# Layer 0 of a two-layer encoder: values first, rotary tables built once per frequency, first weights through ScalarE's queue

## Chip, cores, metric

One core of one Trainium2 chip. The metric is the device time of one execution in microseconds (us), the median of several runs. Engines are named as in the profile: PE (TensorE matmul), PEld (its weight loads), DVE (VectorE), ACT (ScalarE), POOL (GpSimd), SP (SyncE, which issues most DMAs).

## The reference

Batch 1, 256 tokens, width 2048, two layers. Each layer normalizes, projects once, runs two head groups and adds the output projection to the residual:

```python
for l in range(DEPTH):
    h = rms_norm(x, norm_g[l])
    proj = jnp.einsum('btd,dc->btc', h, w_in[l])
    rw_in, g_rw, q, k_at, v_at, g_at = jnp.split(proj, col_splits, axis=-1)
    rw_in = bidir_token_shift(rw_in, shift_mu[l])
    r, k, v, xw, xa = jnp.split(rw_in, rw_splits, axis=-1)
    y_rw = rwkv7_branch(r, k, v, xw, xa, ...)          # scans in both directions, 16 heads of 64
    qh = rope(q.reshape(B, T, AT_HEADS, HEAD_DIM), positions)
    kh = rope(k_at.reshape(B, T, AT_KV_HEADS, HEAD_DIM), positions)
    vh = v_at.reshape(B, T, AT_KV_HEADS, HEAD_DIM)
    y_at = window_attention(qh, kh, vh, sink[l])       # |i-j| <= 128, 4 kv heads, 16 query heads
    mix = jnp.concatenate([y_rw * silu(g_rw), y_at * silu(g_at)], axis=-1)
    x = x + jnp.einsum('btc,cd->btd', mix, w_out[l])
return rms_norm(x, final_g)
```

`rope` needs the sine and cosine of position times one of 32 frequencies, for every token.

## The kernel before

**Weights.** Each weight tile is read as 128x1024 `raw` (SP's queue, three buffers), split by ACT into `hi` (L253) and by DVE into the rest `lo` (L255), 512 columns at a time, two buffers of each. X is split likewise into `XH` (ACT L217) and `XL` (DVE L218), with the norm's gain `G0` multiplied in. A *step* multiplies one 128-row block of a tile by X in three matmuls (L331 to L333, or L600 to L602 for the attention values, where X is the stationary operand). An input tile of 128 columns has 16 steps, the values 32, so a layer has 864 input steps, then 256 output steps.

**The stream.** `S.add` queues a tile's steps, `S.run(n)` emits the next n; `S.later(n, f)` calls f after n more steps. When two steps of a half tile are left, the next half's split is emitted. Only PE keeps the order in which the program is written; DVE, ACT and SP instructions are placed by a scheduler by priority, and those called through `PA` and `PV` keep their order among themselves.

**Layer 0's start.** Eleven matmuls on zeros (L1185) warm PE up. The first tiles are the decay input (`xw`) and the in-context-rate input (`xa`). After the 16 X tiles the squares are summed into `ACC` (four 1024-wide squares on ACT, three adds on DVE), and `norm.add` (L230) turns ACC into the norm by matmuls with a column of ones, eight of them. `norm.spread` (L238) gives the row `rb` that evacuations multiply by.

**Windows.** A layer then runs 13 windows of 64 steps in 11 slots each; between the steps of a slot, generators are advanced. Window w starts head pair w (tiles k, v, r, gate): `scan_p(w)` prepares it, `scan_i` (windows w+2, w+3) builds an inverse in small matmuls, whose pieces pass through ACT (`QF`, `tt`) and DVE (`tv`), `scan_b` (w+3, w+4) runs the scan. The value, key, query and gate tiles of the attention follow the pairs. The generator `attend()` has 17 pieces, placed by `ATT`: `scores(j)` (matmuls into `pscr`, softmax on DVE and ACT into a buffer of tag `mv`), `flip(j)` (transposes `ppt`), `values(j)` (matmuls `po`). In layer 0 the generator `setup()` is advanced at the slots of `ROT`: masks and constants, and then the rotary angles, reduced to a small range in many 128x256 DVE instructions, one piece each, in windows 2 to 7; ACT makes `SIN` and `COS` in window 7.

Of the kernel before, what the change touches and what calls it, by code (L numbers as in the profile page):

```python
# [133 lines left out]
def hybrid_trunk_kernel(ctx, tc, xT, wi, wv, wo, par, fing, dup, iup, sink, pos, cst, out):  # L134
# [209 lines left out]
    SY.dma_start(out=first_w[0][:, 0:512], in_=wi[0, 0, 0, :, 0:512])
    SY.dma_start(out=G0, in_=par[0, :, P_NG : P_NG + NKT])
# [18 lines left out]
    COS = cp.tile([128, T], F32, name="COS")  # L364
    SIN = cp.tile([128, T], F32, name="SIN")

    def setup():
# [6 lines left out]
        for l in range(DEPTH):  # L374
            s = DP[:, l, 0:NSH]
            V.tensor_tensor(s, PR[:, l, P_MU0 : P_MU0 + NSH], PR[:, l, P_MU1 : P_MU1 + NSH], op=ALU.add)
# [30 lines left out]
        def reduce_by(dst, src, period, bits, shift):  # L407
            PV.tensor_scalar(nn, src, 1.0 / period, shift, op0=ALU.mult, op1=ALU.add)
            yield
            PV.tensor_scalar(nn, nn, MAGIC, MAGIC, op0=ALU.add, op1=ALU.subtract)  # L410
            yield
# [893 lines left out]
```

## Time and profile before

| what | value |
|---|---|
| median of 3 runs | 1169.26 us (1168.23 to 1169.78) |
| the profiled execution's own time | 1168.46 us |
| its span, first to last instruction | 1166.7 us |
| mean granted PE clock | 0.994 |
| PE, DVE, ACT busy share | 98%, 79%, 67% |

A row of stretches reads: from:to in us, length, then busy us and instruction count of PE, PEld, DVE, ACT, POOL, then the granted PE clock, the DMA engines' busy share and GB/s. A timeline row reads: start, duration, engine, line, operation, tile written <- tiles read, shape, count, and in brackets the idle time before it and what ended it. Matmuls overlap in the pipeline: a 128x256 one lasts 0.28 us in the record while they start 0.12 apart.

### The profile page before, as it was taken

How to read it: one execution, taken by the hardware profiler on the slowest of the kernel's cores; microseconds unless marked ns; L12 is line 12 of the kernel's file. 1: busy time of each engine (PE TensorE's matmuls, PEld its weight loads, DVE VectorE, ACT ScalarE, POOL GpSimd, SP SyncE). 2: the span in 40 equal slices, each digit the busy share in tenths (PEclk: the TensorE clock that was granted, in tenths of full speed). 3: DMA queues.
4: the chain of work that ended last, by engine and by line, in shares of the span. 5: the costliest groups of instructions: out<-in, count | busy, mean ns of one | idle time of the engine just before them, and what ended most of it. 6: DMA issues, size and time to landing. Idle time of an engine off the chain costs nothing.

```text
span 1166.7 us, 37155 instructions
## 1 busy us (share of the span) xinstructions
PE 1145.5 (98%) x15671; PEld 1051.1 (90%) x15671; DVE 915.9 (79%) x2042; ACT 785.6 (67%) x1986; POOL 21.7 (2%) x23
## 2 busy tenths in 40 slices
PE   8999999999999999999999999999999999999996
PEld 7998999999899998988899889999999999988885
DVE  7889978888877677767768888888887767786665
ACT  6667876787775666655556677876786666675553
POOL 0000000000000000000000000000000000000000
PEclk9999999999999999999999999999999999999998
DMA  7544434333334443477655443334333344345663
GB/s 261 169 152 134 131 103 130 97 112 111 101 116 123 126 127 122 133 235 242 217 182 171 143 136 116 100 114 126 104 112 112 120 130 130 101 150 184 211 202 126
DMA packets 60551, 166.59 MB, mean 143 GB/s; under 512 B 7744, under 2 KB 22880, under 8 KB 60384
## 3 DMA queue, kind: packets, MB, share of 16 engines
q1 hardware_dynamic: 60384, 164.21, 45.1%
q8 instruction: 123, 2.02, 0.7%
q14 instruction: 44, 0.36, 0.1%
HBM read 157.37 MB, written 4.19 MB: 138 GB/s over the span
## 4 chain that ended last, share of the span: by engine, by line
PE 76%; issue 13%; DVE 5%; ACT 4%; DMA 2%; SPq 0%; POOL 0%; POOLq 0%; DVEq 0%; ACTq 0%
PE pm L331 17%; PE pm L333 14%; PE pm L332 14%; PE pm L324 4%; PE pg L855 3%; PE pm L325 2%; PE pcc L1018 2%; DVE lo L255 2%; PE pcc L1046 2%; PE pd L962 1%; PE py L1030 1%; PE py L1003 1%; PE pq L953 1%; PE pcc L1036 1%; ACT hi L253 1%
## 5 line engine op out<-in xcount | busy, mean ns | idle before, releaser
L255 DVE TENSOR_TENSOR lo<-raw,hi 128x512 fp32r<-128x512 f32 x560 | 371.9, 686 | 103.7 <-ACT hi L253 101.6
L253 ACT ACTIVATE hi<-raw 128x512 fp32r<-128x512 f32 x560 | 329.5, 625 | 167.8 <-PE pm L324 58.4
L331 PE MATMUL pm<-XHa,hi 128*128 128x256 f32 x832 | 245.5, 295 | 0.9 <-ACT VA L609 0.4
L331 PE MATMUL pm<-XHb,hi 128*128 128x256 f32 x832 | 243.6, 293 | 0.2 <-ACT hi L253 0.2
L333 PE MATMUL pm<-XHb,lo 128*128 128x256 f32 x832 | 234.0, 281 | 1.4 <-DVE lo L255 1.4
L333 PE MATMUL pm<-XHa,lo 128*128 128x256 f32 x832 | 234.2, 281 | 1.1 <-DVE lo L255 0.8
L332 PE MATMUL pm<-XLa,hi 128*128 128x256 f32 x832 | 234.2, 282 | 0.5 <-DVE XLa L218 0.3
L332 PE MATMUL pm<-XLb,hi 128*128 128x256 f32 x832 | 234.0, 281 | 0.1
L331 PEld LDWEIGHTS pm<-XHa,hi 128*128 128x128 f32 x832 | 157.0, 189 | 11.6 <-ACT XHa L217 1.7
L324 PE MATMUL pm<-M,hi 128*128 128x512 f32 x480 | 166.9, 392 | 0.4 <-ACT hi L253 0.4
L331 PEld LDWEIGHTS pm<-XHb,hi 128*128 128x128 f32 x832 | 157.2, 189 | 5.9 <-ACT hi L253 0.4
L333 PEld LDWEIGHTS pm<-XHa,lo 128*128 128x128 f32 x832 | 157.2, 189 | 2.4 <-DVE lo L255 2.3
L333 PEld LDWEIGHTS pm<-XHb,lo 128*128 128x128 f32 x832 | 157.2, 189 | 2.1 <-DVE lo L255 2.0
L332 PEld LDWEIGHTS pm<-XLa,hi 128*128 128x128 f32 x832 | 157.3, 189 | 1.1 <-DVE XLa L218 1.1
L332 PEld LDWEIGHTS pm<-XLb,hi 128*128 128x128 f32 x832 | 157.3, 189 | 0.3 <-DVE XLb L218 0.3
L325 PE MATMUL pm<-M,lo 128*128 128x256 f32 x480 | 134.3, 280 | 0.2 <-DVE lo L255 0.2
L324 PEld LDWEIGHTS pm<-M,hi 128*128 128x128 f32 x480 | 90.1, 188 | 21.2 <-issue 0.8
L325 PEld LDWEIGHTS pm<-M,lo 128*128 128x128 f32 x480 | 90.1, 188 | 0.5 <-DVE lo L255 0.5
L1041 ACT ACTIVATE suv<-pcc 64x128 f32<-64x128 f32 x128 | 34.5, 270 | 72.3 <-PE pcc L1039 48.5
L1124 ACT ACTIVATE mv<-mv,mx 128x257 f32<-128x257 f32 x56 | 28.0, 502 | 15.1 <-DVE mx L1121 15.0
L956 ACT ACTIVATE QF<-pq 128x256 f16<-128x256 f32 x80 | 30.4, 380 | 10.5 <-PE pq L920 6.2
L855 PE MATMUL pg<-mv,FR 64*128 64x128 f32 x512 | 37.2, 285 | 0.0
(292 smaller groups left out, 2044.3 us busy)
## 6 DMA issues: line engine op xcount, KB each, us to landing
raw<-wi SPq DMA_DIRECT2D x207, 512.0 KB
raw<-wo SPq DMA_DIRECT2D x64, 512.0 KB
raw<-wv SPq DMA_DIRECT2D x8, 512.0 KB
rrot<-u SPq DMA_DIRECT2D x80, 32.0 KB
vg<-xT SPq DMA_DIRECT2D x16, 128.0 KB
xd<-vg SPq DMA_DIRECT2D x16, 128.0 KB
vg<-xd SPq DMA_DIRECT2D x16, 128.0 KB
g<-dup SPq DMA_DIRECT2D x16, 97.0 KB
```

The source lines that it names most:

```text
L253: A.activation(hi[:, q], raw[:, q], AF.Copy)
L255: V.tensor_tensor(lo[:, q], raw[:, q], hi[:, q].bitcast(F32), op=ALU.subtract)
L324: PE.matmul(pm, wh, m.row(kk), start=(kk == 0), stop=(kk == 15), skip_group_check=True)
L325: PE.matmul(pm[:, 0:T], wl, m.row(kk, 0), start=False, stop=(kk == 15), skip_group_check=True)
L331: PE.matmul(pm, wh, xh, start=(kk == 0), stop=False)
L332: PE.matmul(pm, wh, xl, start=False, stop=False)
L333: PE.matmul(pm, wl, xh, start=False, stop=(kk == 15))
L855: PE.matmul(pg[:, h, c * 128 : (c + 1) * 128], BK[half[h], d, c, 1 - h : 3 - h, :].rearrange("p s j -> p (s j)"), MV[half[h], d, c].rearra ...
L956: A.activation(t_sub(QF), flat4(pq[:, :, 0:128]), AF.Copy)
L1018: PE.matmul(pc[half[h], 0, d, :], GE[h][r, d, ci[d], 0, :], SUV[r, d, ci[d], h, :], start=True, stop=True)
L1041: A.activation(here(h), pc[half[h], 1], AF.Copy)
L1124: A.activation(Sc[:, h, q, 0:257], Sc[:, h, q, 0:257], AF.Exp, scale=0.125, bias=mx[:, q : q + 1], accum_out=den[:, q : q + 1])
```

## The change

Four things move together, and then the windows and their tables are laid out anew:

- In layer 0 the four value tiles come first, then xw and xa, then pair 0. Each X tile now serves two value steps (one per 128 tokens), and the evacuation of the values waits 23 steps. xw and xa go to the two halves of one `ps_w` bank pair. In layer 1 the values come right after xw and xa. So 64 steps precede window 0 instead of 32, and 12 windows of 64 and one of 32 follow.
- The first half tile of values and G0 are issued on ACT's queue.
- `setup()` keeps program order throughout (`PV`, `PA`). Positions are loaded as 32x64 quarters, so that partitions hold 4 blocks of tokens times 32 frequencies: the angles are 128x64 instead of 128x256, the sine's and the cosine's arguments are reduced together as 128x128, one Sin makes both, and 16 small DMAs spread the table to `TRIG` (128 x 2 x 256). The Sin stands in window 1; the copies in windows 2 and 3.
- ACC is folded twice more on DVE (to 512 and to 256 columns), and `norm.add` takes one sum instead of four: two matmuls instead of eight, after step 50.

```diff
 ATT = [
-    [3, 9],
-    [1, 3, 5, 6, 8, 10],
-    [0, 2, 4, 5, 6, 8, 9, 10],
+    [9],
+    [1, 4, 8],
+    [0, 2, 3, 5, 6, 8, 9],
+    [0, 1, 2, 3, 4],
 ]
-ROT = {0: [2, 3], 1: [], 7: [2, 5, 7], 8: [1, 3], 9: []}
+ROT = ([2, 4, 6, 7, 9], [3], [3, 5, 8], [2, 6], [5])
...
-    SY.dma_start(out=first_w[0][:, 0:512], in_=wi[0, 0, 0, :, 0:512])
-    SY.dma_start(out=G0, in_=par[0, :, P_NG : P_NG + NKT])
+    A.dma_start(out=first_w[0][:, 0:512], in_=wv[0, 0, :, 0:512])
+    A.dma_start(out=G0, in_=par[0, :, P_NG : P_NG + NKT])
     for a, b in ((0, 2), (2, 4), (4, 8), (8, 12), (12, 16)):
         SY.dma_start(out=X0[:, a:b, :], in_=xT[:, a:b, :])
...
+        if a in (2, 4):
+            SY.dma_start(out=first_w[a // 2], in_=wv[0, a // 2])
...
-        yield from reduce_by(ang, ang, two_pi * 4096.0, 7, 0.0)
-        for dst, shift, add in ((SIN, 0.0, 0.0), (COS, 0.25, np.pi / 2)):
-            yield from reduce_by(dst, ang, two_pi, 11, shift)
...
+        reduce_by(AN[:, 0:1], AN[:, 0:1], two_pi * 4096.0, 7, nn[:, 0:1], (0.0,))
         yield
+        reduce_by(table, AN[:, 0:1].to_broadcast([128, 2, 64]), two_pi, 11, nn, (0.0, 0.25))
+        PV.tensor_scalar(table[:, 1], table[:, 1], float(np.pi / 2), None, op0=ALU.add)
+        PV.tensor_scalar(table, table, PI_IN, -PI_IN, op0=ALU.min, op1=ALU.max)
+        yield
+        PA.activation(table, table, AF.Sin)
...
+        for i, q in enumerate(quarter):
+            for r in quarter:
+                SY.dma_start(out=TRIG[r, :, i * 64 : (i + 1) * 64], in_=table[q])
+            yield
...
+        turns = [(k, b) for k in range(4) for b in range(2)] if l == 0 else [(k, b) for b in range(2) for k in range(4)]
+        done = (lambda: S.later(23, v_evac)) if l == 0 else v_evac
...
         if l == 0:
-            inproj(0, lambda pm: S.later(29, lambda: xw_evac(pm)), raws=first_w, bank=lambda: wbank("pm")[:, 0:T])
-            inproj(1, lambda pm: S.later(13, lambda: xa_evac(pm)))
+            values_in()
...
+            inproj(0, lambda pm: S.later(13, lambda: xw_evac(pm)), bank=lead_bank(0))
+            inproj(1, lambda pm: S.later(4, lambda: xa_evac(pm)), bank=lead_bank(1))
         else:
             inproj(0, xw_evac)
             inproj(1, xa_evac)
+            values_in()
...
-            Sc = t["S"] = st("ge", [2, 2, 264], bufs=2) if j == 2 else st("mv", [2, 2, 264], bufs=3)
+            Sc = t["S"] = hold("s0b", F32, "S0", (2, 2, 264)) if j == 0 else st("mv", [2, 2, 264], bufs=3)
...
-        window(64, *scans(NP + 2), (att, ATT[0]))
-        window(64, *scans(NP + 3), (att, ATT[1]))
-        window(64, (att, ATT[2]))
+        for i in range(3):
+            window(64, *scans(NP + 1 + i), (att, ATT[i]))
+        window(32, (att, ATT[3]), groups=len(ATT[3]))
...
-    S.later(20, lambda: L0.norm.add([ACC[:, i * T : (i + 1) * T] for i in range(4)]))
-    S.later(27, lambda: L0.norm.spread())
+    PV.tensor_tensor(ACC[:, 0 : 2 * T], ACC[:, 0 : 2 * T], ACC[:, 2 * T : 4 * T], op=ALU.add)
+    PV.tensor_tensor(ACC[:, 0:T], ACC[:, 0:T], ACC[:, T : 2 * T], op=ALU.add)
+    S.later(18, lambda: L0.norm.add([ACC[:, 0:T]]))
+    S.later(25, lambda: L0.norm.spread())
```

Lines below 47 shift by one and more in the changed file: L253 becomes L254, L217 L218, L268 (everything called through `PA` or `PV`) L269.

ACT at the program's start, before, from its first instruction (`hi` is a weight split, `XH` an X tile, `mv` a sum of squares):

```order
L253 ACT_TABLE_LOAD
L253 ACTIVATE hi<-raw 128x512
L217 ACTIVATE XHa<-X0a,G_87 128x256
L253 ACTIVATE hi<-raw 128x512
L217 ACTIVATE XHa<-X0a,G_87 128x256 x7
L253 ACTIVATE hi<-raw 128x512 x2
L217 ACTIVATE XHb<-X0b,G_87 128x256 x8
L253 ACTIVATE hi<-raw 128x512 x2
L268 ACTIVATE mv<-X0a 128x1024 x2
```

ACT at the same place, now:

```order
L345 DMA raw<-wv 128x512
L346 DMA G_88<-par 128x16
L254 ACT_TABLE_LOAD
L254 ACTIVATE hi<-raw 128x512
L218 ACTIVATE XHa<-X0a,G_88 128x256
L254 ACTIVATE hi<-raw 128x512
L218 ACTIVATE XHa<-X0a,G_88 128x256 x3
L254 ACTIVATE hi<-raw 128x512 x2
L218 ACTIVATE XHa<-X0a,G_88 128x256 x4
L254 ACTIVATE hi<-raw 128x512 x2
L218 ACTIVATE XHb<-X0b,G_88 128x256 x8
L254 ACTIVATE hi<-raw 128x512 x4
```

Two DMA issues stand ahead, six weight splits instead of four are done before the last eight X tiles, and four more come before the squares.

DVE after the last X tiles, before (`lo` is a weight split, `mv` an add into ACC, `DP` a derived parameter of `setup()`):

```order
L218 SCALAR_TENSOR_TENSOR XLb<-X0b,G_87,XHb 128x256 x8
L255 TENSOR_TENSOR lo<-raw,hi 128x512 x2
L268 TENSOR_TENSOR mv<-mv 128x1024
L376 TENSOR_TENSOR DP<-PR 128x26
L379 TENSOR_SCALAR DP<-PR 128x8
L268 TENSOR_TENSOR mv<-mv 128x1024
L255 TENSOR_TENSOR lo<-raw,hi 128x512 x2
L268 TENSOR_TENSOR mv<-mv 128x1024
```

DVE there, now, up to the norm's first instruction (`rt`):

```order
L219 SCALAR_TENSOR_TENSOR XLb<-X0b,G_88,XHb 128x256 x8
L256 TENSOR_TENSOR lo<-raw,hi 128x512 x4
L269 TENSOR_TENSOR mv<-mv 128x1024 x2
L256 TENSOR_TENSOR lo<-raw,hi 128x512 x2
L269 TENSOR_TENSOR mv<-mv 128x1024
L256 TENSOR_TENSOR lo<-raw,hi 128x512
L269 TENSOR_TENSOR mv<-mv 128x512
L256 TENSOR_TENSOR lo<-raw,hi 128x512
L269 TENSOR_TENSOR mv<-mv 128x256
L269 TENSOR_TENSOR DP<-PR 128x26
L256 TENSOR_TENSOR lo<-raw,hi 128x512
L233 TENSOR_SCALAR rt<-pr 128x2
```

Two more weight splits precede the adds, and two narrow adds stand between later weight splits.

ACT around the sines, before, in window 7 (`suv` belongs to a scan, `QF` and `tt` to an inverse):

```order
L268 ACTIVATE FR<-FR 64x8x64
L1041 ACTIVATE suv<-pcc 64x2x64 x2
L268 ACT_TABLE_LOAD
L268 ACTIVATE SIN<-SIN 128x256
L268 ACTIVATE COS<-COS 128x256
L956 ACTIVATE QF<-pq 128x2x32x4
L924 ACTIVATE tt<-pq 128x2x64x2
```

ACT around the sines, now, in window 1 (`pp` and `ip` are decay factors of pair 0, `kr` an evacuated tile, `th`, `t` and `mf` prepare pairs 0 and 1):

```order
L269 ACTIVATE pp<-FR 128x512
L269 ACTIVATE ip<-FR 128x512
L254 ACTIVATE hi<-raw 128x512 x2
L478 ACTIVATE kr<-u,DP 128x256
L269 ACT_TABLE_LOAD
L269 ACTIVATE KA<-KA 128x128
L254 ACTIVATE hi<-raw 128x512
L269 ACTIVATE th<-th,DP 128x512
L269 ACTIVATE t_973<-kr,PR 128x256
```

The table load and the Sin now stand among weight splits and the preparation of a pair; no piece of an inverse is near.

More of the change, by code (lines that the diff above doesn't have):

```diff
@@ L363, in hybrid_trunk_kernel @@
     SK = cp.tile([128, DEPTH * 16], F32, name="SK")
-    COS = cp.tile([128, T], F32, name="COS")
-    SIN = cp.tile([128, T], F32, name="SIN")
+    TRIG = cp.tile([128, 2, T], F32, name="TRIG")
+    SIN, COS = TRIG[:, 0], TRIG[:, 1]
     def setup():
-        posi = st("t1", [T], I32, bufs=3)
-        SY.dma_start(out=posi, in_=pos.to_broadcast([128, T]))
+        posi = st("t1", [64], I32, bufs=3)
+        quarter = [slice(i * 32, (i + 1) * 32) for i in range(4)]
+        for i, q in enumerate(quarter):
+            SY.dma_start(out=posi[q], in_=pos[:, i * 64 : (i + 1) * 64].to_broadcast([32, 64]))
         SY.dma_start(out=FG, in_=fing)
@@ L402, in setup, with reduce_by @@
-        V.tensor_copy(ang, posi)
-        yield
+        AN = st("KA", [6, 64])
+        ang, nn, table = AN[:, 0], AN[:, 2:4], AN[:, 4:6]
+        PV.tensor_copy(ang, posi)
         PV.tensor_scalar(ang, ang, C[:, C_OFF["inv"] : C_OFF["inv"] + 1], None, op0=ALU.mult)
         yield
[L407 to L411, printed above, removed]
+        def reduce_by(dst, src, period, bits, n, shifts):
+            for i, shift in enumerate(shifts):
+                PV.tensor_scalar(n[:, i], src[:, 0], 1.0 / period, shift, op0=ALU.mult, op1=ALU.add)
+            PV.tensor_scalar(n, n, MAGIC, MAGIC, op0=ALU.add, op1=ALU.subtract)
@@ L589, in rope_evac @@
             return evac
-        pvs = []
-        def v_step(kk, b):
-            def f(w):
-                if not pvs:
-                    pvs.extend(ps_main.tile([128, T], F32, tag="m", name="pva") for _ in range(2))
-                k = kk % 4
-                wh, wl = (x[:, k * 256 : (k + 1) * 256] for x in w)
-                tb = slice(b * 128, (b + 1) * 128)
-                PE.matmul(pvs[b], L.XH[:, kk, tb], wh, start=(kk == 0), stop=False)
-                PE.matmul(pvs[b], L.XH[:, kk, tb], wl, start=False, stop=False)
-                PE.matmul(pvs[b], L.XL[:, kk, tb], wh, start=False, stop=(kk == 15))
-            return f
-        def v_evac():
-            L.VA = st("VA", [2, 256])
-            with tc.high_priority(offset=PRIO_B):
-                A.activation(L.VA[:, 0, :], pvs[0], AF.Copy, scale=L.norm.rt[:, 0:1])
-                V.tensor_scalar(L.VA[:, 1, :], pvs[1], L.norm.rt[:, 1:2], None, op0=ALU.mult)
-        for qt in range(4):
-            S.add(
-                lambda qt=qt: wsplit(wload(wv[l, qt])),
-                [v_step(qt * 4 + k, b) for k in range(4) for b in range(2)],
-                v_evac if qt == 3 else None,
-            )
         def k_place(m):
@@ L1190, in hybrid_trunk_kernel @@
         x_split(L0.XH, L0.XL, X0[:, k, :], k, 0)
-        S.run(1)
+        S.run(2)
+        if k == 11:
+            SY.dma_start(out=C, in_=cst[:, 0:C_KEEP])
+            SY.dma_start(out=PR, in_=par.rearrange("l p n -> p l n"))
     ACC = st("mv", [4 * T], bufs=3)
@@ L1215, in hybrid_trunk_kernel @@
         if l + 1 < DEPTH:
[L1216 removed]
+            S.run(64)
     end.norm.add(end.sums)
```

104 lines of the change are left out of this document (65 added, 39 removed).

## Prediction

> **What bounds the kernel.** I read the page first. TensorE is busy almost throughout, so a gain can come only from places where it waits or runs slowly.
>
> ```profile
> PE 1145.5 (98%) x15671; PEld 1051.1 (90%) x15671; DVE 915.9 (79%) x2042; ACT 785.6 (67%) x1986; POOL 21.7 (2%) x23
> ```
>
> Second, busy time by stretch, one stretch for each window of 64 weight steps (a step is three 128x256 matmuls). Layer 0's windows 0, 1, 5 and 7 and the sum of its thirteen come first, then layer 1's windows 0, 1, 5, 7 and sum. Both layers run the same work there, except that layer 0 also runs `setup()`, and in window 0 its norm.
>
> ```profile
> 23.70:50.20 26.50, 26.50 (x229) 26.50 (x228) 21.50 (x58) 16.36 (x34) 0.81 (x1) 1.00 0.62 201
> 50.20:77.40 27.20, 26.05 (x227) 25.24 (x225) 25.76 (x49) 19.22 (x43) 0.00 (x0) 1.00 0.50 158
> ...
> 187.20:228.10 40.90, 40.39 (x752) 37.32 (x751) 35.07 (x76) 30.51 (x82) 1.31 (x1) 1.00 0.37 113
> ...
> 268.20:311.50 43.30, 41.49 (x753) 38.52 (x751) 35.65 (x75) 33.86 (x86) 1.31 (x1) 0.96 0.37 115
> ...
> sum 471.80, PE 467.39 PEld 433.44 DVE 387.29 ACT 334.12 POOL 10.52; mean PE 35.95 PEld 33.34 DVE 29.79 ACT 25.70 POOL 0.81
> ```
> ```profile
> 599.30:623.50 24.20, 24.20 (x208) 24.20 (x207) 17.15 (x33) 14.57 (x30) 0.00 (x0) 1.00 0.61 184
> 623.50:651.10 27.60, 26.04 (x227) 25.23 (x225) 25.62 (x48) 19.22 (x43) 0.00 (x0) 1.00 0.51 156
> ...
> 760.60:800.50 39.90, 39.90 (x752) 37.06 (x752) 34.03 (x71) 30.40 (x82) 1.31 (x1) 1.00 0.37 112
> ...
> 840.50:880.30 39.80, 39.80 (x752) 36.97 (x751) 34.70 (x73) 30.42 (x82) 1.31 (x1) 1.00 0.37 113
> ...
> sum 465.10, PE 462.81 PEld 429.56 DVE 375.74 ACT 328.77 POOL 9.63; mean PE 35.60 PEld 33.04 DVE 28.90 ACT 25.29 POOL 0.74
> ```
>
> Layer 1 is the control: window 7 costs 3.5 us more in layer 0 (43.3 against 39.8), window 5 1.0 more, window 1 0.4 less. Third, the timeline and stretches around window 7's excess. The step is read here too: twelve matmuls start from 291.83 to 293.12, so 0.117 us each and 0.352 a step.
>
> ```profile
> 291.83 0.28 PE L331 MATMUL pm<-XHa,hi 128*128 128x256 f32 x1
> ...
> 293.12 0.28 PE L333 MATMUL pm<-XHa,lo 128*128 128x256 f32 x1
> 295.21 0.30 PE L962 MATMUL pd<-QF,tt 64*64 64x32 f16 x16 [1.81 <-ACT tt L924]
> ```
> ```profile
> 292.47 1.28 ACT L268 ACT_TABLE_LOAD   x1
> 293.76 0.42 ACT L268 ACTIVATE SIN<-SIN 128x256 f32<-128x256 f32 x1
> ```
> ```profile
> 292.50:295.90 3.40, 1.59 (x40) 1.37 (x38) 3.19 (x9) 3.36 (x10) 0.00 (x0) 1.00 0.25 61
> 295.90:299.30 3.40, 3.40 (x25) 3.24 (x21) 2.61 (x8) 3.36 (x11) 0.00 (x0) 0.50 0.25 101
> ```
>
> ScalarE loads a table and makes the sines just when the inverse needs `tt`; TensorE stands for 1.81 us, and then runs 3.4 us at a granted clock of 0.50, which costs another 1.7.
>
> Fourth, the start: timeline rows in time order by engine, then stretches (all engines; then the third matmul of each step alone, L333, whose count gives the steps; one record lies across a boundary).
>
> ```profile
> 0.74 0.38 SPq L344 DMA_DIRECT2D raw<-wi  x1
> 1.18 0.42 SPq L345 DMA_DIRECT2D G<-par  x1
> 5.46 0.55 PE L1185 MATMUL warm<-QF 128*128 128x512 f16 x1
> 6.37 0.38 PE L331 MATMUL pm<-XHa,hi 128*128 128x256 f32 x1 [0.36 <-ACT XHa L217]
> 8.96 1.71 ACT L217 ACTIVATE XHa<-X0a,G 128x256 fp32r<-128x256 f32 x4 [0.75 <-DMA X0a<-xT]
> 10.57 1.13 ACT L253 ACTIVATE hi<-raw 128x512 fp32r<-128x512 f32 x2
> 12.43 3.25 DVE L218 SCALAR_TENSOR_TENSOR XLb<-X0b,G,XHb 128x256 fp32r<-128x256 f32 x8
> 15.60 1.28 DVE L255 TENSOR_TENSOR lo<-raw,hi 128x512 fp32r<-128x512 f32 x2
> 15.85 1.99 ACT L268 ACTIVATE mv<-X0a 128x1024 f32<-128x1024 f32 x2
> 17.88 1.22 DVE L268 TENSOR_TENSOR mv<-mv 128x1024 f32<-128x1024 f32 x1 [1.00 <-ACT mv L268]
> 19.02 0.18 DVE L376 TENSOR_TENSOR DP<-PR 128x26 f32<-128x26 f32 x1
> 21.09 0.38 PE L333 MATMUL pm<-XHb,lo 128*128 128x256 f32 x1 [1.22 <-DVE lo L255]
> 25.19 1.84 PE L230 MATMUL pr<-C,mv 128*128 128x1 f32 x16
> ```
> ```profile
> 5.00:10.00 5.00, 4.09 (x16) 2.22 (x14) 2.87 (x7) 3.38 (x8) 0.00 (x0) 0.92 0.97 351
> 10.00:15.00 5.00, 4.91 (x29) 4.68 (x28) 4.96 (x12) 5.00 (x13) 0.00 (x0) 0.74 1.02 411
> ```
> ```profile
> 16.20:23.93 7.73, 4.71 (x17) 3.04 (x17) 1.00 0.57 191
> 23.93:37.46 13.53, 8.96 (x33) 6.03 (x33) 1.00 0.54 186
> ```
>
> Today 32 steps are done at 23.93 and 64 at 37.46. At 0.352 a step, 64 steps are 22.5 us; the rest is the 6.37 before the first step, waits, and the norm.
>
> **The front, worked out.** The old order gives TensorE one step (0.352) for each tile of X, while ScalarE spends 1.71/4 = 0.43 on it and VectorE 3.25/8 = 0.41. Values first gives two steps (0.70) a tile. Split costs are 0.57 (ScalarE) and 0.64 (VectorE) per 512 columns, so 32 value steps need about 11.4 us on ScalarE, 11.7 on VectorE, 11.3 on TensorE: balanced, and more bytes are wanted early, 4.1 MB before the last value step.
> The first matmul cannot come before the eleven warm matmuls end at 6.01: that gain is at most 0.36. The transfer that completes the first 1.55 MB ended a wait at 8.96 (X tiles 4 to 7; now it is the second half-megabyte of values). At 411 GB/s each further 0.52 MB takes 1.28. Moving two issues to ScalarE's queue brings X forward by nothing to 0.80 (0.38+0.42); I take 0.4, the middle. Then land: weights at 8.55, X4-7 9.85, weights 11.1, X8-15 13.7, weights 15.0, and after C and PR (0.46 MB, some of it in small packets) the decay tile at 17.5.
> ScalarE then does 4 X tiles 9.85-11.55, split to 12.7, 8 X tiles to 16.0, split to 17.15. VectorE's last value `lo` halves end at 17.25 and 17.9. Four steps follow each half: 17.25+1.3, then 1.4 more, so 32 steps are done near 20.0 instead of 23.93.
> Next, the squares come later than today. ScalarE: decay split 17.5-18.65, three squares to 21.6, half a split, the fourth square to 23.1. VectorE: adds of 1.22 until 23.0, `lo` to 23.6, where TensorE wants it at 23.05: wait 0.55. The third add ends near 25.6, then two new folds (0.65 and 0.35 by width) between `lo` splits end at 27.8. The norm's matmuls stand at step 50, which TensorE reaches at 26.9: a new wait of 0.9. They fall from eight to two, 1.84 to 0.46. The remaining 14 steps and the spread's matmuls bring step 64 to about 34.4. That is 3.1 earlier; I book 2.7, since C and PR's small packets may delay the decay tile. Ends: 1.0 (that delay at a further 2 us) and 4.5 (0.80 of shift, no wait at the norm).
>
> The Trainium skill ("DMA: Bandwidth & Descriptors", Issuing engines are not separate DMA queues) says that issuing from several engines only saves the sequencer's issue time. By that rule the shift would be the whole 0.80, and the sum -6.3 instead of -5.9; no run yet shows ScalarE's queue here.
>
> **Windows 1 to 7.** The layers' differences in window sums are 471.8-465.1 = 6.7, of which window 0 has 2.3 (norm and late evacuations, booked above). The remaining 4.4 lie in windows 1 to 7 and should go, since the sines leave the stretch in which inverses run: -4.4.
>
> The Trainium skill ("TensorE: Matmul & The Clock Gate", What you observe and the table of states) puts the return to half clock after at least one idle window of about 3.4 us. By that rule the 1.81 us stall would cost itself alone, and the sum would be -4.2. The trace disagrees: 0.50 was granted after a stretch that was busy 1.59 of 3.40 us.
>
> **What comes back.** The sines now stand in window 1, where no inverse runs, behind the split of half 16. ScalarE loads the table (1.28), works on 128 instead of 512 columns, and loads back later. Behind it wait the next weight splits. It is hidden if the split runs a half (2.8 us) ahead; at worst it costs 1.81+1.7 as above. I take 0.6.
> Seventeen angle instructions enter window 0 on VectorE, at 0.18 each (the DP row is nearest in width): up to 3.1, less the band cast that leaves. 21.5 busy becomes about 24 of a window that shrinks to some 24.5, and window 1 is already at 25.76 of 27.2. Ends: 0 and 2.4; I take 0.8, because splits have priority.
> SyncE gets 19 more issues (16 table copies, 3 for positions), 0.4 each. It mostly waits for buffers, as the first row shows, so I cost them at nothing; if a copy waited for late sines, the weight loads behind it would start late.
>
> ```profile
> SPq L245 <- DVE lo L255: 477.1, 164, 7.7
> ...
> PE pm L331 <- ACT VA L609: 0.4, 2, 0.2
> ```
>
> The second row is TensorE's wait for a value evacuation. In layer 0 the values' banks now come free at step 55, before step 65 wants them: -0.2. Layer 1 keeps its wait.
> Attention starts one window earlier and its end is denser, 32 steps for five pieces. The tightest score today, in timeline rows:
>
> ```profile
> 480.99 0.39 PE L1109 MATMUL pscr<-KA,kr 64*128 64x256 f32 x2
> ...
> 486.65 0.62 DVE L1127 TENSOR_SCALAR mv<-mv,den 128x256 f32<-128x256 f32 x2
> ...
> 492.59 0.60 PE L1136 MATMUL ppt<-C,mv 128*128 128x128 f32 x4
> ```
>
> It is ready 5.3 us before its transposes. Four slots become three, each of 6.4 steps (2.25) plus about 1.1 of small matmuls: 10.1 instead of 11.6, slack near 3.8. I cost it at 0, ends -0.5 and +2.
>
> Sum: -2.7 - 4.4 + 0.6 + 0.8 - 0.2 = -5.9. The profiled execution took 1168.46 (span 1166.7); it becomes 1162.6. The median of the three runs is 1169.26, 0.8 above it, so the forecast there is 1163.4.
>
> **Rivals.** (1) The sines stall TensorE in window 1 as they did in window 7: 3.5 instead of 0.6, +2.9 on the forecast, 1166.3. For it: the load is as long, VectorE there is 95% busy. Against: no `tt` is awaited there. (2) The front gains nothing: bytes, squares and the folds hold step 64 at 37.4. For it: the 0.97-1.02 DMA share from 5 to 15 us. Against: twice the matmuls per X tile. 1166.1. (3) The other side: attention becomes bound by latency. If window 11's seven pieces and the five of window 12 crowd VectorE so that the 5.3 us slack falls below zero, each of seven transposes in two layers waits; at 0.9 us each that is +12.6, giving about 1176. It decides once the lost slack passes 5.3 plus 0.4 a transpose (0.43 x 14 equals the gain of about 6). Against it: VectorE is below 80% over the span. (4) The change of order does nothing but shift the same waits: sines' 4.4 gone, the same lost at window 0 and 1 on VectorE; 1167 to 1169.
>
> **Chances.** Forecast 0.70, (1) 0.10, (2) 0.08, (4) 0.06, (3) 0.06. The range joins the favourable end (-4.5 - 4.4 - 0.2 - 0.5, about 1159.5) with the case of both new waits at their upper parts and a front of 1.0 (about 1168). About 0.2% (2.3 us) is what a measurement can tell from no change, so under 1166.9 counts as faster: the forecast, and most of (1) and (2), 0.83. Same 0.10, slower 0.07.
>
> **What would show it.** First step near 6.0; step 32 near 20 and step 64 near 34.4; two norm matmul pairs of about 0.5 with a wait on VectorE's ACC; layer 0's windows 5 and 7 within 0.3 of layer 1's; no granted 0.50 near 290; transposes of scores without waits. The forecast is wrong if window 0 or 1 grows by over 2 us, or if waits appear before the score transposes.

## The result, and the profile after

The changed kernel takes 1160.55 us (median of 6 executions, 1160.06 to 1161.27); the kernel before, on the same chip, 1168.35 (6 executions). The ratio is 0.9931, 95% interval 0.992 to 0.9941: 8 us less. The profiled execution took 1160.44 with a span of 1158.6, so its span is 8.1 below that of before (1166.7).

The page's line of engines, after:

```profile
PE 1139.9 (98%) x15659; PEld 1046.6 (90%) x15659; DVE 914.3 (79%) x2038; ACT 783.9 (68%) x1985; POOL 22.2 (2%) x23
```

The busy times hardly move, so the gain lies in waits and in the clock. Stretches by window come next, layer 0 and then layer 1: the windows 0, 1, 2, 4, 5 and 7 and the sum of layer 0; 1, 2, 4 and the sum of layer 1. Both layers now have twelve windows of 64 steps and one of 32.

```profile
33.90:58.10 24.20, 24.20 (x208) 24.20 (x207) 22.20 (x60) 16.02 (x35) 0.00 (x0) 1.00 0.54 174
58.10:84.80 26.70, 26.15 (x227) 25.34 (x225) 25.65 (x48) 21.81 (x46) 0.00 (x0) 1.00 0.57 172
84.80:118.80 34.00, 33.07 (x449) 30.33 (x447) 29.45 (x57) 24.54 (x55) 0.00 (x0) 1.00 0.45 136
...
155.20:196.10 40.90, 40.41 (x753) 37.29 (x751) 34.30 (x72) 30.53 (x82) 1.38 (x1) 1.00 0.33 100
196.10:236.00 39.90, 39.90 (x753) 37.05 (x751) 34.03 (x71) 30.42 (x82) 1.31 (x1) 1.00 0.38 115
...
275.90:315.80 39.90, 39.90 (x752) 37.05 (x751) 34.71 (x73) 30.43 (x82) 1.31 (x1) 1.00 0.36 113
...
sum 453.70, PE 451.40 PEld 418.02 DVE 376.66 ACT 327.70 POOL 9.71; mean PE 34.72 PEld 32.16 DVE 28.97 ACT 25.21 POOL 0.75
```
```profile
627.10:654.80 27.70, 26.01 (x226) 25.19 (x225) 25.64 (x48) 19.25 (x43) 0.00 (x0) 1.00 0.51 156
654.80:687.90 33.10, 32.59 (x448) 30.06 (x447) 29.20 (x56) 24.27 (x55) 0.00 (x0) 1.00 0.43 136
...
724.40:764.30 39.90, 39.90 (x753) 37.05 (x751) 34.05 (x71) 30.42 (x82) 1.31 (x1) 1.00 0.34 105
...
sum 453.20, PE 450.69 PEld 417.79 DVE 368.85 ACT 322.74 POOL 9.65; mean PE 34.67 PEld 32.14 DVE 28.37 ACT 24.83 POOL 0.74
```

The 6.7 us by which layer 0 was longer than layer 1 have shrunk to 0.5. Windows 5 and 7 equal layer 1's 39.9. What is left over stands in windows 2 (34.0 against 33.1) and 4 (40.9 against 39.9), and window 1 is 1.0 shorter than layer 1's, although the Sin is in it. Its table load, on ScalarE, with TensorE waiting neither for it nor for the Sin behind it:

```profile
66.40 1.28 ACT L269 ACT_TABLE_LOAD   x1
```

The start: timeline rows of TensorE (first matmul, third matmul of step 32, waits), two rows of VectorE (the last fold and the weight split behind it) and the two issues on ScalarE's queue; then two stretches.

```profile
5.82 0.39 PE L531 MATMUL pva<-hi,XHa 128*128 128x256 f32 x1
...
19.58 0.28 PE L533 MATMUL pva<-hi,XLb 128*128 128x256 f32 x1
23.29 0.39 PE L334 MATMUL pm<-XHb,lo 128*128 128x256 f32 x1 [0.38 <-DVE lo L256]
...
27.21 0.58 PE L231 MATMUL pr<-C,mv 128*128 128x1 f32 x4 [0.30 <-issue]
...
32.48 0.39 PE L332 MATMUL pm<-XHb,hi 128*128 128x256 f32 x1 [0.59 <-DVE u L477]
...
26.70 0.42 DVE L269 TENSOR_TENSOR mv<-mv 128x256 f32<-128x256 f32 x1
...
0.73 0.40 ACTq L345 DMA_DIRECT2D raw<-wv  x1
1.16 0.45 ACTq L346 DMA_DIRECT2D G<-par  x1
```
```profile
5.00:10.00 5.00, 4.59 (x27) 3.25 (x25) 4.10 (x8) 4.29 (x10) 0.00 (x0) 1.00 0.99 388
10.00:15.00 5.00, 4.90 (x38) 4.70 (x39) 5.00 (x13) 5.00 (x13) 0.00 (x0) 1.00 1.04 414
```

Step 32 starts its third matmul at 19.58 (23.66 before), step 64 at 33.87 (37.19 before). In the second stretch TensorE now has the full clock, where it had 0.74 before. So both half-speed stretches of before, that at 296 us and that near 10 us, are gone. The one near 10 us varies between executions: of the three profiled ones with the old front it lasts 3.4 us in this kernel before, is absent in one of the experiments below (rotary part alone) and lasts 6.8 us in another (positions later). None of the eleven with the new front has it.

By steps the 8.1 us divide so: 3.3 up to step 64; 3.6 in windows 1 to 7 (the seven add up to 257.67 here, 261.30 before); 0.9 in the rest of layer 0's windows; 0.25 in the output steps between the layers; 0.4 in layer 1's input steps, where the value evacuation's wait (0.2 in each layer before) no longer appears; and 0.4 is lost at the program's end. The last three are no larger than their spread over the fourteen profiled executions: what follows layer 1's input steps, for instance, takes between 102.2 and 102.7 us, whatever the edit.

### The profile page after: what moved, and what is told of

The parts are those of the page before. It is cut to its first block, busy times and chain, and to the rows that moved or that the text cites. A ratio compares the mean times of both kernels' runs of the same rounds, so it can differ in the third digit from the quotient of the medians.

```text
span 1158.6 us, 37145 instructions
## 1 busy us (share of the span) xinstructions
PE 1139.9 (98%) x15659; PEld 1046.6 (90%) x15659; DVE 914.3 (79%) x2038; ACT 783.9 (68%) x1985; POOL 22.2 (2%) x23
## 4 chain that ended last, share of the span: by engine, by line
PE 74%; issue 12%; DVE 6%; ACT 4%; DMA 3%; POOL 0%; SPq 0%; POOLq 0%; DVEq 0%; ACTq 0%
PE pm L332 16%; PE pm L333 14%; PE pm L334 13%; PE pm L325 4%; PE pg L877 3%; DVE lo L256 3%; PE pm L326 2%; PE pcc L1040 2%; DMA raw<-wi 2%; PE pcc L1068 1%; PE py L1052 1%; PE pd L984 1%; PE py L1025 1%; PE pcc L1058 1%; PE pq L975 1%
## 5 line engine op out<-in xcount | busy, mean ns | idle before, releaser
L254 ACT ACTIVATE hi<-raw 128x512 fp32r<-128x512 f32 x560 | 329.8, 625 | 171.8 <-PE pm L325 61.3
L332 PEld LDWEIGHTS pm<-XHa,hi 128*128 128x128 f32 x832 | 156.5, 188 | 10.9 <-issue 2.2
L986 DVE CAST_PREDICATED tv<-LV,pd 128x256 f16<-128x256 uint8 x80 | 34.3, 429 | 3.3 <-PE pd L984 2.7
```

Source lines behind the costliest of these rows:

```text
L254: A.activation(hi[:, q], raw[:, q], AF.Copy)
L332: PE.matmul(pm, wh, xh, start=(kk == 0), stop=False)
L986: V.copy_predicated(t_sub(TC), t_mask, flat4(pd[:, :, 0:128]))
```

## The experiments

The runs were made in three groups, each on one chip with the kernel before timed beside them (1169.11, 1168.39 and 1167.98 us). So ratios to it are compared, and 0.001 of ratio is 1.17 us. "Step 64" is when the third matmul of that step starts, and "windows 1-7" the sum of these windows of layer 0, both in the profiled execution.

| kernel | median, us | ratio (95%) | step 64 | windows 1-7 | window 8 |
|---|---|---|---|---|---|
| before | 1168.35 | 1 | 37.19 | 261.30 | 38.90 |
| changed | 1160.55 | 0.9931 (0.9920-0.9941) | 33.87 | 257.67 | 38.84 |
| Sin in window 7, slot 7 | 1166.95 | 0.9985 (0.9975-0.9994) | 33.83 | 258.66 | 43.97 |
| the same, no table load | 1165.92 | 0.9968 (0.9956-0.9981) | 34.67 | 257.12 | 43.99 |
| Sin in window 7, slot 2 | 1159.91 | 0.9933 (0.9919-0.9946) | 34.30 | 256.87 | 38.80 |
| first issues on SP | 1161.56 | 0.9930 (0.9917-0.9942) | 35.19 | 257.16 | 38.83 |
| four sums | 1160.97 | 0.9929 (0.9915-0.9942) | 34.73 | 257.33 | 39.04 |
| rotary part alone | 1169.73 | 1.0013 (1.0005-1.0022) | 43.87 | 257.16 | 38.90 |
| rotary alone, positions later | 1166.18 | 0.9982 (0.9973-0.9991) | 38.72 | 257.69 | 38.90 |
| front alone | 1166.32 | 0.9984 (0.9974-0.9993) | 36.74 | 261.66 | 38.76 |
| xw at offset 16 | 1160.27 | 0.9932 (0.9920-0.9945) | 34.38 | 257.41 | 38.84 |
| two operations on GpSimd | 1158.67 | 0.9919 (0.9906-0.9933) | 34.86 | 256.24 | 38.84 |
| both of these | 1159.89 | 0.9928 (0.9916-0.9940) | 34.68 | 256.34 | 38.85 |
| GpSimd, xw at offset 17 | 1159.43 | 0.9925 (0.9912-0.9937) | 33.06 | 256.42 | 38.82 |

### Does the place of the Sin matter?

```diff
-ROT = ([2, 4, 6, 7, 9], [3], [3, 5, 8], [2, 6], [5])
+ROT = ([2, 4, 6, 7, 9], [], [3], [], [], [], [], [7, 8, 8, 9, 9], [0])
-        PA.activation(table, table, AF.Sin)
-        yield
         PV.tensor_copy(band, cin[:, 0:512])
         yield
+        PA.activation(table, table, AF.Sin)
+        yield
```

> The changed kernel (1160.55 us) with its Sin and the pieces that follow from it put back to window 7 of layer 0; the band's piece goes ahead of it into window 4, the copies into window 7, the product with the sign into window 8. The front, the values and layer 1 stay as in the changed kernel. Theory A (the one angle chain costs time where the band matmuls' releases run on ScalarE, as in window 7 of the kernel before): window 7 grows from 39.9 us to about 42.5 to 43.5, the granted clock falls to 0.50 for 3.4 us there again, which is +2.6 to +3.6; window 4 loses its sign product and may give back up to 0.9. Sum +1.7 to +3.6, 1162.3 to 1164.2 us. Theory B (the place of the Sin is free, and what was gained in windows 1 to 7 came from fewer table operations on VectorE): window 7 stays at 39.9 to 40.3, the clock does not fall, 1160.0 to 1161.0 us.

1166.95 us, beyond both theories. (The band's piece stands in window 2, slot 3, as the diff has it, not in window 4.) Window 7 has the stall, though a smaller one than theory A gave and with the clock at full: 41.56 us instead of 39.91. ScalarE's rows there, TensorE's at the end of the stall, and the stretch behind it:

```profile
305.24 1.28 ACT L269 ACT_TABLE_LOAD   x1
306.53 0.31 ACT L269 ACTIVATE KA<-KA 128x128 f32<-128x128 f32 x1
...
308.50 0.38 ACT L946 ACTIVATE tt<-pq 128x256 f16<-128x256 f32 x1
```
```profile
308.93 0.30 PE L984 MATMUL pd<-QF,tt 64*64 64x32 f16 x16 [1.51 <-ACT tt L946]
```
```profile
309.00:312.00 3.00, 3.00 (x53) 2.83 (x54) 2.78 (x7) 2.79 (x8) 0.00 (x0) 1.00 0.13 25
```

The larger part, 5.1 us, is in window 8, and the rows of SP's queue tell why; under them is the ScalarE row that took the late load.

```profile
296.59 4.74 SPq L246 DMA_DIRECT2D raw<-wi  x2
306.86 11.36 SPq L431 DMA_DIRECT2D TRIG<-KA  x16
318.32 6.46 SPq L246 DMA_DIRECT2D raw<-wi  x4
```
```profile
322.13 0.63 ACT L254 ACTIVATE hi<-raw 128x512 fp32r<-128x512 f32 x1 [4.38 <-DMA raw<-wi]
```

The first copy of the table sat at the head of SP's queue until the Sin was done; from 306.86 the sixteen copies hold the queue for 11.4 us, and no weight load was issued from 301.3 to 318.3. TensorE then stood 3.6 us, for VectorE's `ge` (324.34), which stands behind the two late weight splits there; and from 325.40 it ran 3.4 us at a granted clock of 0.50, which costs another 1.6. VectorE had also waited 4.7 us for the table itself (until 319.52), but stood idle once more, for 2.06 us, until the late split came: so the load is what ended last.

The same kernel without a table load there (`AF.Tanh` for `AF.Sin`; the tables then hold tanh):

> As the run before it (the angle chain in window 7), with tanh in place of sine, so that the rotary tables hold other values and ScalarE changes no function table there. Theory A (the price in window 7 is the 1.28 us table load together with the operation behind it): the stall goes, window 7 is 39.9 to 40.4 us, the clock stays at full, 1159.7 to 1161.0 us. Theory B (any 0.3 us of extra ScalarE work between two band activations stops TensorE as long): window 7 stays within 0.5 us of the run before it. Theory C (the place is free anyway): both runs are equal to the changed kernel.

Window 7 is 40.16 us, 1.40 less than with the load and 0.25 above the undisturbed 39.91: theory A for window 7. Window 8 stays at 43.99, and so the time, 1165.92 us, is outside theory A's range: the copies' price has nothing to do with the table load.

The Sin in the same window, but in slot 2, with the copies in slots 5 to 8:

```diff
-ROT = ([2, 4, 6, 7, 9], [], [3], [], [], [], [], [7, 8, 8, 9, 9], [0])
+ROT = ([2, 4, 6, 7, 9], [], [3], [], [], [], [], [2, 5, 6, 7, 8], [0])
```

> As the run with the Sin in window 7 (1166.95 us), with the Sin moved from slot 7 to slot 2 of that window and the copies to its slots 5 to 8, so that the copies no longer wait long for it. Theory A (window 8's 5.1 us came from SP: the first copy waited 5.8 us for the table, and the weight load behind it came 4.4 us late; window 7's 1.65 us is the table load ahead of the band's activations): window 8 falls from 43.97 to 38.9 or 39.3, window 7 stays between 40.2 and 41.8, 1161.0 to 1162.2 us. Theory B (the 16 copies in a row on SP, about 7 us of issues, hold back the loads wherever they stand): window 7 or 8 stays 3 us or more longer than in the changed kernel, 1164 us or more.

1159.91 us, below both theories: no price is left at all, and the ratio is that of the changed kernel. Window 7 is 39.86, window 8 38.80. Its rows on ScalarE and on SP's queue:

```profile
286.41 1.28 ACT L269 ACT_TABLE_LOAD   x1
287.70 0.31 ACT L269 ACTIVATE KA<-KA 128x128 f32<-128x128 f32 x1
287.92 0.61 ACT L254 ACTIVATE hi<-raw 128x512 fp32r<-128x512 f32 x1
```
```profile
288.04 10.86 SPq L431 DMA_DIRECT2D TRIG<-KA  x16
```

The load is as long, and the copies hold the queue nearly as long, 10.9 us; but a weight split follows the Sin here, and the copies don't wait for it long: no weight load was issued for 12.2 us (286.83 to 299.00), against 17.0 with the Sin in slot 7, and TensorE waited for none. So it is neither the window nor the load that costs. By these rows it is what stands next behind them: an inverse's `tt` on ScalarE, and on SP the weight loads. The run moves the Sin and the copies together; that each place counts by itself is read from the rows, and for the table load also from the run without it.

### The parts one by one

The rotary part alone: `setup()`, `TRIG` and `ROT` of the changed kernel in the kernel before, whose front and window order stay.

> The kernel before with the rotary part of the change alone: one angle tile for sine and cosine, its setup spread over windows 0, 1, 2 and 4; the front, the order of values and layer 1 are those of the kernel before. Theory A (the parts add): windows 1 to 7 lose what they lost in the changed kernel, 3.6 us, and the drop of the clock at 296 us goes; the front keeps its drop at 9 us; 1168.35 - 3.6 = 1164.7 us, 1164.0 to 1165.3. Theory B (the order of the values in layer 0 made windows 1 to 7 shorter, not the rotary tables): within 1 us of the kernel before, 1167.4 to 1169.4. Theory C (without the new front the pieces collide with setup in windows 0 and 1): slower than 1166.5.

1169.73 us, slower than before: theory C. The windows 1 to 7 do give what the theory of sums says (257.16 against 261.30), but step 64 comes at 43.87 instead of 37.19. Rows of SP's queue in the kernel before, and in this one; then ScalarE's row on which TensorE waits, and the stretches in which TensorE pays:

```profile
9.16 0.49 SPq L369 DMA_DIRECT2D t<-pos  x1
10.21 0.33 SPq L370 DMA_DIRECT2D FG<-fing  x1
11.51 0.33 SPq L371 DMA_DIRECT2D SK<-sink  x1
12.80 0.33 SPq L245 DMA_DIRECT2D raw<-wi  x1
```
```profile
9.36 4.64 SPq L371 DMA_DIRECT2D t<-pos  x4
...
17.25 0.33 SPq L245 DMA_DIRECT2D raw<-wi  x1
...
22.21 4.93 SPq L245 DMA_DIRECT2D raw<-wi  x3
```
```profile
31.23 2.37 ACT L253 ACTIVATE hi<-raw 128x512 fp32r<-128x512 f32 x4 [8.91 <-DMA raw<-wi]
```
```profile
25.00:30.00 5.00, 5.00 (x36) 5.00 (x37) 1.03 (x6) 0.00 (x0) 0.70 (x1) 0.81 0.68 222
30.00:35.00 5.00, 3.74 (x17) 3.22 (x16) 3.07 (x8) 2.30 (x4) 0.00 (x0) 0.50 0.45 143
35.00:40.00 5.00, 5.00 (x32) 5.00 (x32) 3.79 (x10) 3.62 (x10) 0.00 (x0) 0.67 0.51 178
```

While X streams in, SP issues a transfer only every 1.3 us or so, whatever its size. By the profile each of these issues waits until an earlier large transfer has landed: the four of the positions wait 0.8 to 1.4 us each, for X0a, `raw`, X0b and X0b, which were issued eight places ahead of them. Three more transfers of 8 KB put the next weight load 4.45 us later.

That load is still split in time, at 21.18. What TensorE waits for (1.26 us, until 31.91) is the split of the load behind it, whose issue began at 22.21 and held the queue until 26.20; before, it took from 20.87 to 21.29. The larger part of the 6.2 us that steps 32 to 50 lose is the granted clock: 0.50 from 28.10 to 38.34, which costs 5.1. It fell ahead of that wait, just behind the norm's matmuls. Why the one issue took 4.0 us, and why the clock fell there and not in the kernel before, no run shows. That the four transfers are at the root is shown by moving them. In the changed kernel they stand behind two weight loads. With the four moved into window 0,

```diff
-        for i, q in enumerate(quarter):
-            SY.dma_start(out=posi[q], in_=pos[:, i * 64 : (i + 1) * 64].to_broadcast([32, 64]))
...
         yield
+        for i, q in enumerate(quarter):
+            SY.dma_start(out=posi[q], in_=pos[:, i * 64 : (i + 1) * 64].to_broadcast([32, 64]))
         PV.tensor_copy(
             LV.rearrange(
```

> The rotary part of the change alone in the kernel before, as in the earlier run of it that came to 1169.73 us, with one difference: the four small transfers of the positions (8 KB each) are issued in window 0 and no longer ahead of the weight loads of the front. Theory A (the earlier run gained 3.5 us in window 7 and lost 6.2 us at steps 32 to 50, since SP issues one transfer after another, each of the four held the queue for about 1.3 us, and the weight load behind them came 4.5 us later): step 64 falls from 43.9 to between 37.2 and 38.2, window 7 stays at 39.9, 1168.4 - 3.5 = 1164.9 us, 1164.2 to 1165.6. Theory B (the setup pieces on VectorE and ScalarE, now ahead of the front's own work, make the loss): step 64 stays above 42, 1168.5 us or more.

1166.18 us: 3.6 less than with the transfers ahead, and the intervals are apart. Steps 32 to 50 take 8.59 us again (14.76 with the transfers ahead, 8.60 before). It is 1.3 us short of theory A. In the profiled execution the steps up to 32 are 1.5 later than before, and the clock is why in part: it was granted at 0.50 for 6.8 us there, where the kernel before has 3.4.

```profile
10.60:17.40 6.80, 6.40 (x27) 5.89 (x28) 6.39 (x15) 6.80 (x17) 0.00 (x0) 0.50 1.01 379
```

Its executions agree: the three with a mean granted clock of 0.996 or more took 1164.8 to 1165.3 us, within theory A, and the eight others, at 0.993 or 0.994, 1165.3 to 1167.2. Why the clock differs between them is left open.

The other part alone: the changed kernel with the old `setup()`, tables and `ROT`, the old angles in `KA`'s place.

> The changed kernel with the rotary setup of the kernel before (two full tables, made in windows 0 to 8, both Sin in window 7): the values first and the new front alone. Theory A (the parts add): step 64 stays at 33.9 to 34.9, window 7 comes back to 43.3 with the fall of the clock, windows 2 and 4 change by what the rotary pieces make of them (33.3 and 40.0), window 5 gets the 0.9 us: 1160.55 + 3.6 = 1164.2 us, 1163.5 to 1165.0. Theory B (the shorter window 7 comes from the new order of the windows and not from the rotary tables): window 7 stays below 41, 1161.5 us or less.

1166.32 us, 2 more than theory A. Windows 5 and 7 are back at 40.87 and 43.31, the latter with a wait of 1.76 us for `tt` and half clock from 308.99, so theory B falls. But the front loses too. Rows of VectorE and of TensorE near step 61, and the stretch behind the stall there:

```profile
31.23 0.96 DVE L386 CAST LV<-mv 128x1536 uint8<-128x1536 f32 x1 [0.67 <-DMA mv<-cst]
32.11 0.42 DVE L392 CAST band<-mv 128x512 bf16<-128x512 f32 x1
...
34.51 0.42 DVE L474 TENSOR_TENSOR u<-pm,rb 128x256 f32<-128x256 f32 x1
```
```profile
34.98 0.38 PE L332 MATMUL pm<-XHb,hi 128*128 128x256 f32 x1 [2.23 <-DVE u L474]
```
```profile
35.00:40.00 5.00, 5.00 (x29) 5.00 (x30) 4.37 (x15) 2.63 (x6) 0.00 (x0) 0.66 0.38 110
```

The old setup's casts wait on VectorE for the constants, in the midst of the front; ScalarE's next weight split waits 2.0 us for the second of them, and `u` behind is late: 2.2 us, and then half clock for 3.4 us. The new setup spreads these pieces over windows 0 to 2. So the new setup helps the front, and the new front, which puts the positions behind two weight loads, helps the rotary part. Alone the front brings 1.9 us; the rotary part brings 2.1 with the positions out of the way, and loses 1.5 as it stands; together they bring 8.

### The front's small parts

```diff
-    A.dma_start(out=first_w[0][:, 0:512], in_=wv[0, 0, :, 0:512])
-    A.dma_start(out=G0, in_=par[0, :, P_NG : P_NG + NKT])
+    SY.dma_start(out=first_w[0][:, 0:512], in_=wv[0, 0, :, 0:512])
+    SY.dma_start(out=G0, in_=par[0, :, P_NG : P_NG + NKT])
```

> The changed kernel with the two first transfers (first piece of the weight, first piece of the codebook's table) issued by SP again. Theory A (as booked in the prediction: the two issues of about 0.43 us on SP delay those behind them by 0.9 us, but the transfers share the 16 engines with what is behind them anyway): the first matmul stays between 5.8 and 6.4 us, step 64 between 33.9 and 34.7, 0 to +0.8 us, 1160.5 to 1161.4. Theory B (the front's whole gain over the booked sum comes from the queue): first matmul at 6.4, +1.0 us or more. Theory C (the queue costs time, since ScalarE issues ahead of its first activation and table load): -0.3 us or better.

Step 64 is at 35.19, 0.5 to 1.4 later than in the changed kernel and the three others whose front is the same (33.83, 33.87, 34.30, 34.67). Step 32 tells more: 20.86 here, and 19.58 to 20.39 in the ten other kernels with the new front. The times don't separate it (0.9930 against 0.9931). So one execution is later by about the size of theory A, and nothing shows in the time. (G0 is the norm's gain; the expectation's "codebook's table" is a slip.)

```diff
-    PV.tensor_tensor(ACC[:, 0 : 2 * T], ACC[:, 0 : 2 * T], ACC[:, 2 * T : 4 * T], op=ALU.add)
-    PV.tensor_tensor(ACC[:, 0:T], ACC[:, 0:T], ACC[:, T : 2 * T], op=ALU.add)
-    S.later(18, lambda: L0.norm.add([ACC[:, 0:T]]))
+    S.later(18, lambda: L0.norm.add([ACC[:, i * T : (i + 1) * T] for i in range(4)]))
```

> The changed kernel without the two folding additions of the squares on VectorE: the norm's sum over partitions is again made of eight matmuls over the four tiles of squares. Theory A (TensorE's time in the front is what counts): 1.84 instead of 0.46 us of norm matmuls, less a shorter wait of 0.3 to 0.5 us ahead of them: +0.9 to +1.1, 1161.5 to 1161.7 us. Theory B (the front waits for VectorE and the transfers, so the added matmuls fill time that TensorE waits in): within 0.3 us of the changed kernel. Theory C (the folds delay the norm by more than they spare): -0.3 us or better.

In the trace theory A: the norm's matmuls follow without a wait, and steps 48 to 64 take 8.77 us instead of 7.96.

```profile
26.78 1.84 PE L231 MATMUL pr<-C,mv 128*128 128x1 f32 x16
```

The time's interval holds 0 as well as 0.9, so the folds' worth is a reading of the trace, not a measured time.

```diff
-            inproj(0, lambda pm: S.later(13, lambda: xw_evac(pm)), bank=lead_bank(0))
+            inproj(0, lambda pm: S.later(16, lambda: xw_evac(pm)), bank=lead_bank(0))
```

> The changed kernel with the eviction of the second half of xw put at step offset 16 instead of 13, behind the matmuls that write the other half of its two-bank tile. Theory A (the 0.59 us wait at 32.48 us for VectorE's u is a wait of those matmuls for the eviction's read, and of nothing that is needed): it goes, -0.4 to -0.6, 1159.9 to 1160.2 us. Theory B (the wait moves to the next reader of xw): within 0.2 us of the changed kernel.

No gain. It is theory B by size, but the wait did not go to another reader; it moved to the last step of the same matmuls:

```profile
34.04 0.39 PE L332 MATMUL pm<-XHb,hi 128*128 128x256 f32 x1 [0.58 <-DVE u L477]
```

At offset 17, on the kernel with GpSimd below, it is gone:

> The kernel with the band cast and the sign product on GpSimd (1158.67 us), with the eviction of xw's second half at offset 17. At 16 the wait for u did not go: it moved from 32.48 to 34.04 us, from the last four steps to the very last step of the matmuls that write the other half of its tile. Theory A (17 is behind them all): no wait for u ahead of step 64, -0.4 to -0.7 us, 1158.0 to 1158.3. Theory B (VectorE then does the evictions of both halves together, and a weight split behind them comes late in window 0): window 0 grows from 24.3 to 24.9 or more, 1158.7 us or more.

Step 64 is at 33.06, the earliest of all, but window 0 grows from 24.26 to 26.09: theory B. Both halves are then evicted together, and a weight split comes late. Step 128 comes at 59.15, with the offset of 13 at 59.12.

```profile
36.75 0.39 PE L332 MATMUL pm<-XHb,hi 128*128 128x256 f32 x1 [0.56 <-ACT hi L254]
```

### What is left in windows 2 and 4

```diff
-        PV.tensor_copy(band, cin[:, 0:512])
+        G.tensor_copy(band, cin[:, 0:512])
...
-        PV.tensor_scalar(SIN, SIN, C[:, C_OFF["sgn"] : C_OFF["sgn"] + 1], None, op0=ALU.mult)
+        G.tensor_scalar(SIN, SIN, C[:, C_OFF["sgn"] : C_OFF["sgn"] + 1], None, op0=ALU.mult)
```

> The changed kernel with two rotary operations of windows 2 and 4 (the cast of the band and the product of sine and sign) on GpSimd instead of VectorE. Theory A (each delays the releases of window 2 and of window 4 on VectorE by the 0.9 us that these windows have over layer 1's): window 2 falls from 34.0 to 33.2, window 4 from 40.85 to 39.9, -1.7 us, 1158.8 us, 1158.5 to 1159.3. Theory B (the excess of 0.9 us comes from the order in which the pieces push the other instructions, whatever the engine): both windows keep their lengths, 1160.2 to 1160.9. Theory C (GpSimd's operations are much longer than VectorE's and share its access to memory, so that VectorE's releases come later): slower than 1161 us.

1158.67 us. Theory A holds for window 4, which falls from 40.85 to 39.86, and not for window 2, which keeps 33.80. Windows 2 and 4, and GpSimd's two rows:

```profile
85.40:119.20 33.80, 32.90 (x448) 30.25 (x447) 29.30 (x56) 24.45 (x55) 1.47 (x1) 1.00 0.44 137
155.80:195.60 39.80, 39.80 (x752) 36.95 (x751) 34.02 (x71) 30.42 (x82) 1.41 (x1) 1.00 0.34 105
```
```profile
26.88 2.19 POOL L427 CAST band<-mv 128x512 bf16<-128x512 f32 x1 [26.45 <-DMA mv<-cst]
...
86.29 1.47 POOL L433 TENSOR_SCALAR TRIG<-TRIG,C 128x256 f32<-128x256 f32 x1 [55.95 <-DMA TRIG<-KA]
```

They take 2.19 and 1.47 us there, where VectorE took 0.42 and 0.35. The edit moves them in time as well: on GpSimd the cast runs ahead of window 0 and the product in window 2, so it doesn't separate the engine from the place. Window 4 is also 39.9 in the three kernels with the product in window 8, so there the place is enough. Window 2's excess is not the cast, which is gone from it. Nor is it a loss by itself: with window 1 it adds up to 60.65 us in the changed kernel, 60.82 in its layer 1, and 60.8 to 60.9 in the three kernels with the Sin and the copies in window 7. But the cast stands ahead of the norm's `rt` on GpSimd, which comes at 29.12 instead of 28.07; that may be part of the later step 64. The ratio's interval (0.9906 to 0.9933) overlaps that of the changed kernel, so that it beats it by more than the 1 us of window 4 is not shown.

> The two edits of the runs before it together. Theory A (they are in different places and add): -2.1 to -2.3, 1158.2 to 1158.5 us. Theory B (one of them does nothing): 1158.8 or 1160.0 us, whichever is left.

1159.89 us, not below the single edit: the offset of 16 adds nothing, as by itself.

## Why the prediction came out, point by point

The forecast was 1163.4 and a sum of -5.9; the span lost 8.1. The direction and the places were right, most terms were some tenths too cautious, and one reason was wrong.

- **The front** (-2.7, step 64 near 34.4): the forecast counts a step as done at the end of its third matmul, 0.28 behind its start. So step 64 was done at 34.15 in the profiled execution, -3.3, and at 34.1 to 34.95 over the four kernels with that front: a spread of 0.9 that the forecast's 34.4 lies in. Step 32 was forecast near 20.0 and done at 19.86. The decay tile's wait was 0.54 (forecast 0.55); the wait at the norm was only 0.3 to 0.5 instead of 0.9, since the last fold ended at 27.1, not 27.8. What the forecast left out altogether is the half-speed stretch near 10 us, shown in its own rows at 0.74. It is gone, but the rotary part alone, which has the old front and none of it, reaches step 32 at 24.18 (start of the third matmul), so it is not shown that it cost the old front anything. The wait that it did not see is the 0.59 at 32.48: xw's eviction reads one half of a tile while xa's matmuls write the other. That step 64 came out so near is in part luck: from the norm on the forecast has 6.6 us (27.8 to 34.4), the rows have 6.2 without that wait, and the wait filled the rest.
- **Two issues on ScalarE's queue** (0.4 of 0 to 0.8): with both issues back on SP, step 64 was 0.5 to 1.4 later. The first matmul came at 5.82 instead of 6.37, below the floor of 6.01 that the forecast took from the warm matmuls, because these ended at 5.73; with both issues on SP they ended at 6.09, and the first matmul came at 6.11. So that start is not the queue's. The Trainium skill ("DMA: Bandwidth & Descriptors", Issuing engines are not separate DMA queues) has only the issue time to save, here 0.80; the trace agrees, as far as a spread of 0.9 can tell.
- **Windows 1 to 7** (-4.4): -3.6 net of all that came back. The reason given, that the sines leave the stretch in which inverses run, is the step that failed. In the same stretch they cost nothing in slot 2, and 1.65 us in slot 7. What counts, by the rows, is whether an inverse's `tt` is next behind them on ScalarE, as it was before. Nor was window 5's 1.0 the angles' work as such: it moved to window 4, where one product of 0.35 us on VectorE stands, and it goes when that product stands elsewhere.
- **The Sin in window 1** (+0.6) and **the angle work in window 0** (+0.8): both nothing. Window 1 is 26.65 (layer 1: 27.68), window 0 24.26 (24.41), although VectorE's busy time in it rose to 22.20. Instead window 2 is 0.9 longer than in layer 1, which had no term; window 1 makes up for it.
- **SyncE's 19 more issues** (0): right in the changed kernel, but by its order alone. The rotary part alone lost 3.6 us (6.2 in its trace) by the four for the positions at the wrong place, and sixteen of them behind a late Sin held back the loads as the prediction's "if" says, for 3.6 us of TensorE and 1.6 more at half clock. "It mostly waits for buffers" is an average over the span; in the front it waits for earlier transfers to land.
- **Layer 1 keeps its wait** for the value evacuation: wrong. With the values right behind xw and xa, its 0.2 us went there too, and layer 1's input steps are 0.4 shorter.
- **Attention** (0): right. The tightest score had slack near 3.8 in the forecast; it ends at 480.39 and its transposes start at 484.40, so 4.0.
- Of the rivals, (1), (3) and (4) did not happen. (2) is nearly what the front does in combination with the old setup: step 64 at 36.74.
- The upper end of the range does not follow from its own bounds: with a front of 1.0 and both new waits at 3.5 and 2.4 the sum gives 1169.6, not 1168. Nothing came near it.

## To carry to other kernels

Before moving an expensive step, list what stands directly behind it on its engine, on the DMA queue that its result feeds, and who waits for that; a few slots earlier in the same window can be free where this one costs 6 us. Small transfers count by their number and place in the issuing queue, not by their bytes: look at what load they delay. Two parts of a change that are worth 2 us each by themselves can be worth 8 together, when each removes the other's obstacle, so a part that fails alone is not yet refuted.
